# Down product in groups of 3, 4 and 4 blocks, its tiles laid out ahead of the last up pair, and the low parts of its first two items made between that pair's conv taps

## The chip, the cores and the metric

The kernel runs on one core of a Trainium2 chip. The metric is the time of one execution in device microseconds (us); lower is better. The version before the change takes 1487.21 us, the median of three runs (1486.26 to 1487.37).

A core has five engines that run their own instruction queues in order and wait for one another by semaphores: TensorE (PE; PEld is its weight load), VectorE (DVE), ScalarE (ACT), GpSimd (POOL) and SyncE (SP, here only a queue for DMA transfers).

## The reference

One layer of a streaming encoder over 1024 positions plus 16 meta tokens: attention and a state-space branch, then a gated feed-forward part with a causal depthwise convolution, then a final norm. The change lies in the last two, whose core is this:

```python
def _conv_ffn(xn, w_up, conv_w, conv_b, w_down):
    seq_len = xn.shape[1]
    hid = xn @ w_up
    hp = jnp.pad(hid, ((0, 0), (CONV_WIDTH - 1, 0), (0, 0)))
    conv = conv_b + sum(hp[:, j:j + seq_len] * conv_w[j] for j in range(CONV_WIDTH))
    val, gate = jnp.split(conv, 2, axis=-1)
    return (jax.nn.silu(gate) * val) @ w_down
...
        h = h + _conv_ffn(xn, w_ffn_up[layer], ffn_conv_w[layer], ffn_conv_b[layer],
                          w_ffn_down[layer])
    h = _rmsnorm(h, norm_final_g)
    return h[:, N_META:]
```

All is float32; `D_MODEL` is 1024 and `D_FF` 2816, so `w_up` has 2 x 2816 columns and `w_down` 2816 rows.

## The kernel before

**Split operands.** Float32 products are made of three matmuls. Each operand is split into a high part (a copy by ACT, rounded to the matmul's type) and a low part, the difference between the operand and the high part (`split_lo`, L127, on DVE or POOL). This difference is called a cut below. PE then adds high x high, high x low and low x high in PSUM.

**The up product** makes 22 pairs of 128 gate and 128 value rows. Pairs 0 and 21 are done plainly (`plain_pair`), pairs 1 to 20 by a seven-product scheme (`block_pair`). In a plain pair, three blocks of positions are computed for the gate (`og`) and then three for the value (`ov`). Behind each block ACT applies the first conv tap (L1034) and DVE the two others (L1036). `glue` (L1005) applies Silu, multiplies gate and value (on POOL, for the last pair on DVE, L1007), and writes the 128 rows to `a_d` in DRAM (from SP's queue, for the last pair from ACT's, L1008). While the up product runs, POOL also prepares sums of the down weights, `t_d`.

**The down product** takes the 22 x 128 rows of `a_d` as 11 blocks of two, and multiplies them by `w_down` with a Strassen-Winograd scheme of seven products, made in `ORDER` = (0, 4, 1, 2, 5, 3, 6). The blocks are worked off in groups: two blocks, then three, three and three. An item is one product of one group. For each item and block `forms` (before: L1142 to L1170) makes two operands: one from quarter tiles of `a_d` (`ar`, sometimes after a sum on POOL, L1151 to L1157), one from a weight tile (`wr`). Each is copied by ACT (L1163) and cut (L127), on POOL for products 0, 4 and 5 and on DVE for 1, 2, 3 and 6. The results lie in 14 operand slots: six of their own (`op0` to `op5`) and eight in the tiles `xhi` and `xlo`, which are free once the up product has ended.

`product` (L1206) then runs four tiles of 128 positions; per tile every block gives three matmuls of 512 columns (L1219 to L1221). PSUM banks are `m`, `m`, `m`, `po` or `s`, `t`, `s`, `t` in turn, and products 4, 5 and 6 add to the banks of 0, 1 and 3. Behind each tile its bank is drained: copied by ACT for the very first product (L1224), else added by DVE (L1226) to `hs` (the residual and result, read from `h_d`) or to a helper `u`. In the last group the norm follows: `square` (L1192: square and sum on ACT, `va` on DVE, L1195) and `finish` (L1198: a power on POOL, L1200, scaling on DVE, L1201, and ACT, L1203, then the write). The last tile of the last item is done in two pieces, of 288 and 224 columns, in one bank.

**What sets the order.** The program text gives the dependencies, and a scheduler sets the order of instructions on each engine at build time; `after(a, b)` (L122) puts `a` behind `b` on their engine or behind its end without data between them. `prepare` (L1253) prepares as many items ahead as the 14 slots allow. Before the change the pool `down1` with the first tiles of the down product is opened behind the last up pair (L1115), the rest (`dn`) further on, so the loads of the first blocks wait for the tiles of the up product to be freed. `first_copy` and `first_add` hold the cuts of group 0 behind certain drains, and `behind` puts loads behind those of `hs`.

Of the kernel before, what the change touches and what calls it, by code (L numbers as in the profile page):

```python
# [47 lines left out]
def block_kernel(ctx, tc, x, meta, g1, w_q, w_k, w_v, w_f, w_u, w_g, b_f, w_ao, lam_d, bw_d, cw_d,  # L48
# [912 lines left out]
    ha = pool(st_r, "hid", side="right")  # L961
# [20 lines left out]
    def combine(a, b, op):  # L982
        f_ = rp.tile([P, KH, P], F, tag="sf", name="sf", bufs=2)
        sums.append(GP.tensor_tensor(f_, a, b, op))  # L984
        return f_
# [19 lines left out]
    def glue(g_, v_, c):  # L1005
        S.activation(g_, g_, AF.Silu)  # L1006
        (V if c == NFF - 1 else GP).tensor_tensor(v_, v_, g_, ALU.mult)  # L1007
        (S if c == NFF - 1 else SY).dma_start(a_d[P * c:P * c + P], v_)  # L1008
# [4 lines left out]
    def plain_pair(c):  # L1013
# [3 lines left out]
        for m, tag in ((NFF + c, "og"), (c, "ov")):  # L1017
            raw = up_raw(m)
            w2 = [split_q(raw[:, KH * q:KH * q + KH]) for q in range(2)]
            if last:  # L1020
                o = ha.tile([P, SEQ], F, tag="h", name=tag, bufs=3, padded_shape=[P, LQ + 2])
            else:
                o = conv_out(m, tag)
            for t, n in QBLK:
# [9 lines left out]
                S.activation(o_, ps[:, :w], AF.Identity, bias=cwc(3, m), scale=cwc(0, m))  # L1034
                for j in (1, 2):
                    V.scalar_tensor_tensor(out=o_, in0=ps[:, j:w + j], scalar=cwc(j, m), in1=o_,  # L1036
                                           op0=ALU.mult, op1=ALU.add)
# [69 lines left out]
    st_t.close()  # L1107
    plain_pair(NFF - 1)
# [4 lines left out]


    down1 = pool(ctx, "down1", side="left")  # L1115
    small = [down1.tile([P, 4, 512], R, name=f"op{q}") for q in range(4)]
# [3 lines left out]
    dpool = {}  # L1120
    pairs = {}

    h_load = []

    def raw_tile(j, k, h_):
        if (k, h_) not in pairs.setdefault(j, {}):
            pairs[j][k, h_] = dpool[j % 4 // 2].tile([P, 512], F, tag=f"a{k}{h_}", name="ar", bufs=2)
        return pairs[j][k, h_]

    def behind(ld, j, p=None):  # L1130
        if h_load and (j in groups[1] or p in (2, 5, 3, 6) and j in groups[0]):
            after(ld, h_load[3 if p == 2 else -1])

    def load_pair(j):
        for k in range(2):
            c0 = P * (2 * j + k)
            for h_ in range(2):
                behind(SY.dma_start(raw_tile(j, k, h_), a_d[c0:c0 + P, 512 * h_:512 * h_ + 512]), j)

    n_op = [0]  # L1140
    own_w = {0: (0, 0), 4: (1, 0), 6: (1, 1)}

    def forms(p, j):
        r = pairs[j]
        b_ = down1.tile([P, 512], F, tag="w", name="wr", bufs=8)
        behind(SY.dma_start(b_, w_block(*own_w[p], j) if p in own_w else t_d[p][P * j:P * j + P]), j, p)

        a11, a21, a12, a22 = (r[k, h_] for k in range(2) for h_ in range(2))
        sub, add = ALU.subtract, ALU.add
        if p == 1:  # L1150
            GP.tensor_tensor(a11, a11, a21, sub)  # L1151
        elif p == 2:
            GP.tensor_tensor(a11, a22, a11, add)
        elif p == 3:
            GP.tensor_tensor(a21, a22, a21, sub)
        elif p == 6:
            GP.tensor_tensor(a11, a11, a12, sub)  # L1157
        slot = ops[n_op[0] % len(ops)]
        n_op[0] += 1
        a_ = (a11, a11, a11, a21, a12, a22, a11)[p]  # L1160
        eng = GP if p in (0, 4, 5) else V
        for q, src in ((0, a_), (2, b_)):
            hi = S.copy(slot[q], src)  # L1163
            if first_copy and j < 2 and p >= 5:
                after(hi, first_copy[1])
            cut = split_lo(eng, slot[q + 1], src, slot[q])
            cuts.setdefault((p, j), []).append(cut)
            if first_add and eng is V and j < 2 and p > 2:
                after(cut, first_add[1 if p == 3 else 3])
        return slot  # L1170

    first_add, first_copy = [], []
    cuts = {}

# [31 lines left out]
    def product(g, p, slots, first, last):  # L1206
        l_, r_ = HALF
        joins = p in JOINS
        for t, bk in enumerate(banks(g, p)):
# [5 lines left out]
            for c0, n in parts:  # L1215
# [7 lines left out]
                if first and p == 0:  # L1223
                    first_copy.append(S.copy(to, ps))  # L1224
                else:
                    first_add.append(V.tensor_tensor(to, to, ps, ALU.subtract if p in MINUS else ALU.add))  # L1226
                    if (g, p, t) == (1, 0, 3):
                        for cut in cuts[1, 3] + cuts[1, 4]:
                            after(cut, first_add[-1])
# [473 lines left out]
```

## Time and profile before

| What | Value |
|---|---|
| Time, median of 3 runs | 1487.21 us (1486.26 to 1487.37) |
| Profiled execution, its time | 1486.29 us |
| Profiled execution, its span | 1484.5 us |
| PE busy | 1450.3 us, 98% of the span |
| DVE busy | 1050.5 us, 71% |
| ACT busy | 690.8 us, 47% |
| POOL busy | 664.5 us, 45% |
| Mean granted clock of PE | 0.991 |
| Last matmul of the up product starts | 1248.63 us |
| First matmul of the down product starts | 1248.79 us |
| Last matmul of the down product starts | 1477.21 us |

The span runs from the first to the last instruction of the profiled execution. Times inside the trace count from its start. Durations on the engines come from the trace: "busy" is the sum of the durations of an engine's instructions, and "idle before" is the time in which it had nothing to do just ahead of an instruction, with the instruction that ended it. Instructions overlap at their ends (a matmul of 512 columns is shown as 0.39 us while the next starts after 0.23), so the step from start to start tells the pace. The granted clock is TensorE's share of full speed.

### The profile page before, as it was taken

What the parts mean: (1) busy time and instruction counts of PE and PEld (TensorE: products, weight loads), DVE (VectorE), ACT (ScalarE), POOL (GpSimd) and SP (SyncE); (2) the same over time, 40 slices, a digit from 0 to 9 for tenths busy, and PEclk for the clock granted to TensorE, in tenths of its full rate; (3) what the DMA queues carried; (4) which work ended last, traced back from release to release, by engine and by line L of the source; (5) the groups of instructions that cost most, each with busy time, mean ns of one, the idle gap of its engine ahead of it and who ended that gap; (6) DMA issues with size and microseconds to landing.
All of it is one profiled execution on the core that took longest, in us unless ns stands there. A gap on an engine that the chain in (4) does not pass through costs nothing.

```text
span 1484.5 us, 26303 instructions
## 1 busy us (share of the span) xinstructions
PE 1450.3 (98%) x9681; PEld 1362.9 (92%) x9681; DVE 1050.5 (71%) x2169; ACT 690.8 (47%) x1338; POOL 664.5 (45%) x759
## 2 busy tenths in 40 slices
PE   7999999999999999999999999999999999899997
PEld 6999999988999999999879999999999998678886
DVE  7989377862657676656255888888876665888785
ACT  5355565542646566532046544444444434444343
POOL 2101105741554556525021455555544416779766
PEclk8999999999999999999999999999999999999999
DMA  6455544441120212157134555667543216764412
GB/s 244 105 135 144 157 96 136 143 151 31 37 92 24 80 51 65 44 205 269 69 143 114 128 163 167 183 174 182 143 121 93 86 44 230 260 207 133 141 45 114
DMA packets 83364, 190.96 MB, mean 129 GB/s; under 512 B 13818, under 2 KB 26250, under 8 KB 82884
## 3 DMA queue, kind: packets, MB, share of 16 engines
q1 hardware_dynamic: 67604, 154.77, 31.9%
q0 software_dynamic: 9984, 24.45, 8.9%
q10 hardware_dynamic: 5648, 10.07, 1.9%
q8 instruction: 76, 1.25, 0.3%
q14 instruction: 52, 0.43, 0.1%
HBM read 146.98 MB, written 61.00 MB: 140 GB/s over the span
## 4 chain that ended last, share of the span: by engine, by line
PE 82%; DVE 6%; issue 3%; DMA 3%; ACT 2%; POOL 2%; SPq 0%; POOLq 0%; DVEq 0%; ACTq 0%
PE mm L149 5%; PE mm L148 5%; PE mm L147 5%; PE sp L212 5%; PE sp L211 5%; PE sp L213 5%; PE mm L213 3%; PE mm L211 3%; PE mm L212 3%; PE tp L213 3%; PE tp L211 3%; PE tp L212 3%; PE tp L682 3%; PE po L704 2%; PE po L703 2%
## 5 line engine op out<-in xcount | busy, mean ns | idle before, releaser
L147 PE MATMUL mm<-xhi,whi 128*128 128x342 f32 (+2 forms) x584 | 191.2, 328 | 1.5 <-DVE q L127 1.0
L148 PE MATMUL mm<-xlo,whi 128*128 128x342 f32 (+2 forms) x584 | 189.8, 325 | 1.1 <-DVE xlo L127 0.9
L149 PE MATMUL mm<-xhi,wlo 128*128 128x342 f32 (+2 forms) x584 | 189.6, 325 | 0.0
L1007 POOL TENSOR_TENSOR ov<-ov,og 128x1024 f32<-128x1024 f32 x21 | 51.4, 2449 | 152.7 <-ACT og L1006 151.6
L127 DVE TENSOR_TENSOR sw<-sf,sw 128x512 fp32r<-128x512 f32 x80 | 75.8, 947 | 54.1 <-ACT sw L976 53.8
L147 PEld LDWEIGHTS mm<-xhi,whi 128*128 128x128 f32 x584 | 111.0, 190 | 3.3 <-ACT xhi L178 1.2
L148 PEld LDWEIGHTS mm<-xlo,whi 128*128 128x128 f32 x584 | 111.0, 190 | 2.6 <-DVE xlo L127 1.9
L149 PEld LDWEIGHTS mm<-xhi,wlo 128*128 128x128 f32 x584 | 110.9, 190 | 0.3
L976 ACT CAST sw<-sf 128x512 fp32r<-128x512 f32 x80 | 50.0, 625 | 119.5 <-POOL sf L984 83.1
L984 POOL TENSOR_TENSOR sf<-raw 128x512 f32<-128x512 f32 x40 | 52.4, 1311 | 102.1 <-PE mm L897 53.2
L213 PE MATMUL mm<-xhi,sw 128*128 128x256 f32 (+1 forms) x320 | 90.4, 283 | 0.0
L211 PE MATMUL mm<-xhi,sw 128*128 128x256 f32 (+1 forms) x320 | 90.3, 282 | 0.0
L212 PE MATMUL mm<-xlo,sw 128*128 128x256 f32 (+1 forms) x320 | 90.1, 281 | 0.0
L689 ACT CAST th<-tp 128x256 fp32r<-128x256 f32 (+3 forms) x120 | 56.1, 472 | 60.9 <-PE tp L682 28.2
L127 DVE TENSOR_TENSOR tl<-tp,th 128x256 fp32r<-128x256 f32 (+3 forms) x120 | 65.1, 547 | 26.2 <-ACT th L689 24.8
L976 ACT CAST sw<-raw 128x512 fp32r<-128x512 f32 x68 | 41.9, 621 | 82.7 <-DMA raw<-in_w_up_dram 33.9
L1093 DVE SCALAR_TENSOR_TENSOR ov<-hv,cwt,ov 128x1024 f32<-128x1024 f32 x40 | 78.7, 1969 | 0.1
L984 POOL TENSOR_TENSOR sf<-raw,sf 128x512 f32<-128x512 f32 x40 | 65.1, 1626 | 25.1 <-DVE sw L127 25.1
L654 POOL TENSOR_SCALAR pt<-pt,nm 128x144 f32<-128x144 f32 (+4 forms) x72 | 51.0, 709 | 52.9 <-DVE nm L653 51.8
L652 ACT ACTIVATE pt<-pt,nm 128x144 f32<-128x144 f32 (+4 forms) x72 | 52.9, 735 | 26.7 <-DVE nm L651 26.2
L645 DVE CUSTOM_DVE_ANT_0 pt<-sp,fb 128x328 f32<-128x328 f32 (+8 forms) x112 | 46.4, 430 | 20.6 <-PE sp L640 12.3
L211 PEld LDWEIGHTS mm<-xhi,sw 128*128 128x128 f32 x320 | 60.5, 189 | 0.0
(621 smaller groups left out, 5350.3 us busy)
## 6 DMA issues: line engine op xcount, KB each, us to landing
raw<-in_w_up_dram SPq DMA_DIRECT2D x44, 512.0 KB, 3.6
t_d<-in_w_dn_dram POOLq DMA_DIRECT2D x44, 256.0 KB, 7.0
ar<-a_d SPq DMA_DIRECT2D x44, 256.0 KB, 4.9
wr<-t_d SPq DMA_DIRECT2D x44, 256.0 KB, 3.2
a_d<-ov SPq DMA_DIRECT2D x21, 512.0 KB, 2.6
wr<-in_w_dn_dram SPq DMA_DIRECT2D x33, 256.0 KB, 5.0
t_d<-in_w_dn_dram SPq DMA_DIRECT2D x22, 256.0 KB, 4.5
t_d<-t_d SPq DMA_DIRECT2D x22, 256.0 KB, 4.8
```

Source lines behind the costliest of these rows:

```text
L127: return eng.tensor_tensor(out_, src, hi.bitcast(F), ALU.subtract)
L147: yield PE.matmul(ps, whi[:, i, :], ahi[:, i], start=(i == 0), stop=False)
L148: yield PE.matmul(ps, whi[:, i, :], alo[:, i], start=False, stop=False)
L149: yield PE.matmul(ps, wlo[:, i, :], ahi[:, i], start=False, stop=(i == k - 1))
L211: PE.matmul(ps, a[0][:, i], bh, start=(i == 0 and not joins), stop=False, skip_group_check=True)
L212: PE.matmul(ps, a[0][:, i], bl, start=False, stop=False, skip_group_check=True)
L213: PE.matmul(ps, a[1][:, i], bh, start=False, stop=(i == kh - 1), skip_group_check=True)
L652: S.activation(pt[:n, :kc], pt[:n, :kc], AF.Exp, bias=nm[:n, 1:2], scale=0.125, accum_out=nm[:n, 2:3])
L689: S.copy(th[:kn, z:tw], tp[:kn, z:tw])
L976: S.copy(hi, src)
L984: sums.append(GP.tensor_tensor(f_, a, b, op))
L1093: V.scalar_tensor_tensor(out=o, in0=h_[:, j:SEQ + j], scalar=cwc(j, m), in1=o, op0=ALU.mult, op1=ALU.add)
```

## The change

It has five parts.

1. **Groups.** The blocks are worked off as 3, 4 and 4 instead of 2, 3, 3 and 3.
2. **Layout.** The pools of the up product that are no longer needed (`upf`, `tright`, `hid`) get a stack of their own, `st_f`, closed ahead of the last up pair. `down1` is opened there too, with all tiles that the first items need; the last pair's `og` and `ov` lie in it.
3. **Loads.** Quarter tiles of `a_d` are loaded product by product as they are used (`USES`), not by block; `behind` is gone. The rows of pairs 20 and 21 are written to `a_d` from POOL's queue. All eight `hs` loads stand behind the preparation of the first items.
4. **First items.** The cuts of the first two items, (0, 0) and (0, 4), go to DVE, and `after` puts them and their ACT copies behind the taps of the last up pair's blocks, three to a block, from the second block on. Nine slots are given out, so item (0, 1) is prepared there as well.
5. **Later cuts.** `product` gets the DVE cuts that `prepare` has made and puts a quarter of them behind the drain ahead of each of its four tiles; `first_copy` and `first_add` go.

```diff
+    st_f = ExitStack()
+    fp = pool(st_f, "upf", side="right")
...
-        (S if c == NFF - 1 else SY).dma_start(a_d[P * c:P * c + P], v_)
+        (GP if c >= NFF - 2 else SY).dma_start(a_d[P * c:P * c + P], v_)
...
+                if last:
+                    convs.append((first, tap))
...
     st_t.close()
+    st_f.close()
+    down1 = pool(ctx, "down1", side="left")
...
+    small = op_tiles(3, 6)
+    a_room("11")
+    a_room("01")
+    for tag in ("og", "ov"):
+        down1.tile([P, D], F, tag=tag, name=tag, padded_shape=[P, LQ + 2])
+    for q in range(8):
+        down1.tile([P, 512], F, tag="w", name="wr", bufs=8)
...
     plain_pair(NFF - 1)
...
+    USES = {0: ((0, 0),), 4: ((1, 0),), 1: ((0, 0), (0, 1)), 2: ((1, 1), (0, 0)), 5: ((1, 1),), 3: ((1, 1), (0, 1)),
+            6: ((0, 0), (1, 0))}
+
+    def forms(g, p):
+        early = g == 0 and p in ORDER[:2]
+        eng = GP if p in (0, 4, 5) and not early else V
+        for j in groups[g]:
+            for kh in USES[p]:
+                raw_tile(j, *kh)
...
+            for q, src in ((0, a_), (2, wr[q_])):
+                hi = S.copy(slot[q], src)
+                cut = split_lo(eng, slot[q + 1], src, slot[q])
+                if (g, p) == (0, 5):
+                    after(cut, sums[-1])
+                if early:
+                    i = 2 * len(groups[0]) * ORDER.index(p) + 2 * q_ + q // 2
+                    after(hi, convs[1 + i // 3][0])
+                    after(cut, convs[1 + i // 3][1])
+                if eng is V:
+                    mine.append(cut)
...
-    def product(g, p, slots, first, last):
+    def product(g, p, slots, first, last, cuts):
...
+                    if drains:
+                        for cut in cuts[len(cuts) * t // 4:len(cuts) * (t + 1) // 4]:
+                            after(cut, drains[-1])
+                    drains.append(V.tensor_tensor(to, to, ps, ALU.subtract if p in MINUS else ALU.add))
...
-    groups = [range(0, 2), range(2, 5), range(5, 8), range(8, 11)]
+    groups = [range(0, 3), range(3, 7), range(7, 11)]
...
+    room[0] = 9
+    new = prepare()
...
+    for c in range(KD):
+        SY.dma_start(hs[c], h_d[P * c:P * c + P])
+    room[0] = len(ops) - 9
     for g, p in items:
-        prepare()
-        if (g, p) == (0, 0):
-            for c in range(4, KD):
-                h_load.append(SY.dma_start(hs[c], h_d[P * c:P * c + P]))
+        new = prepare()
```

Up to the last up pair the order on every engine is unchanged. Three places behind that show how instructions move; a row is line, operation and tiles, and lines behind L910 shift by up to some 30 between the two programs.

First, DVE at the end of the last up pair, before. The L1036 rows are the taps of its blocks (`x2`: two in a row), L1007 the multiplication of gate and value, and the L127 rows are cuts of the third item, (0, 1):

```order
L1036 SCALAR_TENSOR_TENSOR ov_14891<-tp_14920,cwt_9276,ov_14891 128x342 x2
L1036 SCALAR_TENSOR_TENSOR ov_14891<-sp_14948,cwt_9276,ov_14891 128x340 x2
L1007 TENSOR_TENSOR ov_14891<-ov_14891,og_14798 128x1024
L1277 MEMSET eps_15035 128x1
L127 TENSOR_TENSOR op4_15033<-ar_14986,op4_15033 128x512
L127 TENSOR_TENSOR op4_15033<-wr_15081,op4_15033 128x512
L127 TENSOR_TENSOR op5_15060<-ar_14994,op5_15060 128x512
L127 TENSOR_TENSOR op5_15060<-wr_15088,op5_15060 128x512
```

The same place after the change; taps are L1040 here, `op3` to `op5` the slots of the second item and `xhi` those of the third:

```order
L1040 SCALAR_TENSOR_TENSOR ov_14928<-tp_14957,cwt_9276,ov_14928 128x342
L127 TENSOR_TENSOR op3_14799<-ar_15040,op3_14799 128x512
L127 TENSOR_TENSOR op4_14800<-ar_15042,op4_14800 128x512
L1040 SCALAR_TENSOR_TENSOR ov_14928<-tp_14957,cwt_9276,ov_14928 128x342
L127 TENSOR_TENSOR op5_14801<-ar_15044,op5_14801 128x512
L127 TENSOR_TENSOR op3_14799<-wr_15046,op3_14799 128x512
L127 TENSOR_TENSOR op4_14800<-wr_15048,op4_14800 128x512
L1040 SCALAR_TENSOR_TENSOR ov_14928<-sp_14985,cwt_9276,ov_14928 128x340
L127 TENSOR_TENSOR op5_14801<-wr_15050,op5_14801 128x512
L127 TENSOR_TENSOR xhi_91<-ar_15016,xhi_91 128x512
L1040 SCALAR_TENSOR_TENSOR ov_14928<-sp_14985,cwt_9276,ov_14928 128x340
L127 TENSOR_TENSOR xhi_91<-wr_15070,xhi_91 128x512
```

Cuts of the second item, which stood on POOL, and of the third now stand between the taps, some of them between the two taps of one block.

Second, DVE in products 2 and 5 of the last group, before. The L1226 rows that change `u` drain product 2, and those that change `hs` drain product 5; L1195 is `va` of the norm:

```order
L127 TENSOR_TENSOR xhi<-ar,xhi 128x512
L127 TENSOR_TENSOR xhi<-wr,xhi 128x512
L1226 TENSOR_TENSOR hs_15072<-hs_15072,po 128x512
L1226 TENSOR_TENSOR u_15066<-u_15066,sp 128x512
L1226 TENSOR_TENSOR u_15067<-u_15067,tp 128x512
L1226 TENSOR_TENSOR u_15068<-u_15068,sp 128x512
L1226 TENSOR_TENSOR u_15069<-u_15069,tp 128x512
L1226 TENSOR_TENSOR hs_15070<-hs_15070,mm 128x512
L1195 SCALAR_TENSOR_TENSOR va<-ss,eps 128x1
L1226 TENSOR_TENSOR hs_15065<-hs_15065,mm 128x512
```

The same place after the change, from the last drain of product 2 on (drains are L1257, `va` is L1223):

```order
L1257 TENSOR_TENSOR u_15130<-u_15130,po 128x512
L127 TENSOR_TENSOR op_14799<-a_16009,op_14799 128x512
L127 TENSOR_TENSOR op_14799<-wr,op_14799 128x512
L1257 TENSOR_TENSOR hs_15123<-hs_15123,sp 128x512
L127 TENSOR_TENSOR op_14800<-ar,op_14800 128x512
L127 TENSOR_TENSOR op_14800<-wr,op_14800 128x512
L1223 SCALAR_TENSOR_TENSOR va<-ss,eps 128x1
L1257 TENSOR_TENSOR hs_15124<-hs_15124,tp 128x512
L127 TENSOR_TENSOR op_14801<-ar,op_14801 128x512
L127 TENSOR_TENSOR op_14801<-wr,op_14801 128x512
```

The last cuts stood ahead of these drains and now stand between them, two to a drain, through both products.

Third, DVE in products 3 and 6 of the last group, where the results are finished (L1201), before:

```order
L1226 TENSOR_TENSOR hs_15072<-hs_15072,tp 128x512
L1201 SCALAR_TENSOR_TENSOR hs_15071<-hs_15071,rs,gfB 128x512
L1226 TENSOR_TENSOR hs_15061<-hs_15061,sp 128x512
L1195 SCALAR_TENSOR_TENSOR va<-ss,va 128x1
L1201 SCALAR_TENSOR_TENSOR hs_15072<-hs_15072,rs,gfB 128x512
L1226 TENSOR_TENSOR hs_15062<-hs_15062,tp 128x512
L1195 SCALAR_TENSOR_TENSOR va<-ss,va 128x1
L1201 SCALAR_TENSOR_TENSOR hs_15061<-hs_15061,rs,gfB 128x512
```

And after the change (`finish` is L1229; `hs_15123` is the first of the eight result tiles here, while above they are numbered from `hs_15061`):

```order
L1257 TENSOR_TENSOR hs_15123<-hs_15123,mm 128x512
L1223 SCALAR_TENSOR_TENSOR va<-ss,va 128x1
L1229 SCALAR_TENSOR_TENSOR hs_15123<-hs_15123,rs,gfB 128x512
L1257 TENSOR_TENSOR hs_15124<-hs_15124,mm 128x512
L1223 SCALAR_TENSOR_TENSOR va<-ss,va 128x1
L1229 SCALAR_TENSOR_TENSOR hs_15124<-hs_15124,rs,gfB 128x512
L1257 TENSOR_TENSOR hs_15125<-hs_15125,mm 128x512
L1223 SCALAR_TENSOR_TENSOR va<-ss,va 128x1
L1257 TENSOR_TENSOR hs_15126<-hs_15126,po 128x512
L1229 SCALAR_TENSOR_TENSOR hs_15125<-hs_15125,rs,gfB 128x512
```

Before, the drain of the next tile stood ahead of a tile's `finish`; now a tile's `finish` mostly stands ahead of the next drain.

More of the change, by code (lines that the diff above doesn't have):

```diff
@@ L982, in combine @@
     def combine(a, b, op):
-        f_ = rp.tile([P, KH, P], F, tag="sf", name="sf", bufs=2)
+        f_ = fp.tile([P, KH, P], F, tag="sf", name="sf", bufs=2)
         sums.append(GP.tensor_tensor(f_, a, b, op))
@@ L1020, in plain_pair @@
             if last:
-                o = ha.tile([P, SEQ], F, tag="h", name=tag, bufs=3, padded_shape=[P, LQ + 2])
+                o = down1.tile([P, SEQ], F, tag=tag, name=tag, padded_shape=[P, LQ + 2])
             else:
@@ L1107, in block_kernel, with op_tiles, a_room @@
     st_t.close()
+    st_f.close()
+    down1 = pool(ctx, "down1", side="left")
+    def op_tiles(a, b):
+        return [down1.tile([P, 4, 512], R, name=f"op{q}") for q in range(a, b)]
+    def a_room(kh):
+        for q in range(3):
+            down1.tile([P, 512], F, tag=f"a{kh}{q}", name="ar")
+    small = op_tiles(3, 6)
[5 more added lines that the diff above has]
+        down1.tile([P, 512], F, tag="w", name="wr", bufs=8)
+    a_room("00")
+    a_room("10")
+    small = op_tiles(0, 3) + small
     plain_pair(NFF - 1)
@@ L1119, in block_kernel @@
             for t_ in (xhi, xlo) for q in range(4)]
-    dpool = {}
-    pairs = {}
-    h_load = []
+    pairs, halves = {}, {}
     def raw_tile(j, k, h_):
         if (k, h_) not in pairs.setdefault(j, {}):
-            pairs[j][k, h_] = dpool[j % 4 // 2].tile([P, 512], F, tag=f"a{k}{h_}", name="ar", bufs=2)
-        return pairs[j][k, h_]
-    def behind(ld, j, p=None):
-        if h_load and (j in groups[1] or p in (2, 5, 3, 6) and j in groups[0]):
-            after(ld, h_load[3 if p == 2 else -1])
@@ L1134, in load_pair @@
[L1134 to L1138, printed above, removed]
+            if j % 4 < 3:
+                t_ = down1.tile([P, 512], F, tag=f"a{k}{h_}{j % 4}", name="ar")
+            else:
+                if k == 0:
+                    halves[j, h_] = (dn.tile([P, D], F, tag="a3", name="a3") if h_ else
+                                     down1.tile([P, D], F, tag="og", name="a3", padded_shape=[P, LQ + 2]))
+                t_ = halves[j, h_][:, 512 * k:512 * k + 512]
@@ L1140, in block_kernel @@
+            c0 = P * (2 * j + k)
+            SY.dma_start(t_, a_d[c0:c0 + P, 512 * h_:512 * h_ + 512])
+            pairs[j][k, h_] = t_
+        return pairs[j][k, h_]
     n_op = [0]
     own_w = {0: (0, 0), 4: (1, 0), 6: (1, 1)}
[L1143 to L1148, printed above, removed]
-        sub, add = ALU.subtract, ALU.add
[L1150 to L1170, printed above, removed]
@@ L1177, in block_kernel @@
+    drains = []
     JOINS = {4: 0, 5: 1, 6: 3}
@@ L1223, in product @@
                 if first and p == 0:
-                    first_copy.append(S.copy(to, ps))
+                    drains.append(S.copy(to, ps))
                 else:
[L1226 to L1229, printed above, removed]
+                    if drains:
+                        for cut in cuts[len(cuts) * t // 4:len(cuts) * (t + 1) // 4]:
+                            after(cut, drains[-1])
+                    drains.append(V.tensor_tensor(to, to, ps, ALU.subtract if p in MINUS else ALU.add))
                 if last and p == 6:
```

76 lines of the change are left out of this document (37 added, 39 removed).

## The prediction

> **What bounds the kernel now.** The page's first part says that TensorE is nearly always busy, so a change can only win where it stands still or runs at a lower clock. The windows view (length, then busy time and count of PE, PEld, DVE, ACT, POOL, then the granted clock) finds that place in the down product.
>
> ```profile
> PE 1450.3 (98%) x9681; PEld 1362.9 (92%) x9681; DVE 1050.5 (71%) x2169; ACT 690.8 (47%) x1338; POOL 664.5 (45%) x759
> ...
> 1248.70:1316.00 67.30, 58.45 (x233) 45.24 (x232) 54.00 (x58) 31.12 (x57) 59.33 (x41) 0.92 0.70 246
> 1316.00:1474.00 158.00, 157.53 (x693) 129.13 (x692) 127.81 (x158) 63.13 (x125) 123.41 (x90) 1.00 0.35 114
> 1380.00:1470.00 90.00, 90.00 (x397) 74.12 (x396) 65.34 (x87) 32.91 (x68) 69.70 (x53) 1.00 0.21 65
> 1308.00:1312.00 4.00, 1.02 (x5) 0.52 (x5) 4.00 (x4) 1.46 (x3) 4.00 (x3) 1.00 0.57 169
> 1312.00:1316.00 4.00, 4.00 (x11) 3.14 (x12) 4.00 (x6) 1.24 (x2) 4.00 (x4) 0.57 0.52 159
> ```
>
> The third window has no pause: 90.00 / 397 = 0.227 us for a matmul of 512 columns. At that pace the first stage's 233 matmuls take 52.9 of its 67.30 us, so **14.4 us are lost there**; the next 693 take 157.3 of 158.00. The waits of PE (total, times, longest) from 1248.7 us on name what ends the pauses:
>
> ```profile
> PE sp L1219 <- DVE u L1226: 3.0, 1, 3.0
> PE sp L1219 <- DVE hs L1226: 2.1, 1, 2.1
> PE tp L1219 <- DVE hs L1226: 1.8, 1, 1.8
> PE mm L1220 <- POOL op L127: 1.7, 1, 1.7
> PE mm L1219 <- ACT xhi L1163: 1.4, 1, 1.4
> PE mm L1219 <- DVE hs L1226: 0.4, 1, 0.4
> ```
>
> All but the 1.8 (the end, below) lie in the first stage. They are low parts not yet made, or drains that stand in DVE's queue behind low parts. The rest of the 14.4 is clock: behind the pause of 3.0 us the window 1312 to 1316 shows clock 0.57, and its 11 matmuls take 4.00 instead of 2.5 us, 1.5 more. The Trainium skill's page "TensorE: Matmul & The Clock Gate", section "What's actually happening", puts the fall to half rate after an idle window of about 3.4 us. The trace shows it after 2.98 us, so the measurement decides; by the page, each 1.5 us that I add for such a fall below would be nothing.
>
> **What the change removes.** A low part is a "cut" (L127). These rows give its price, by whether POOL works beside it, and that of a drain:
>
> ```profile
> 1253.72 0.69 DVE L127 TENSOR_TENSOR op<-ar,op 128x512 fp32r<-128x512 f32 x1 [1.10 <-issue]
> 1254.33 1.79 DVE L127 TENSOR_TENSOR op<-wr,op 128x512 fp32r<-128x512 f32 x1
> 1256.05 1.77 DVE L127 TENSOR_TENSOR op<-ar,op 128x512 fp32r<-128x512 f32 x1
> ...
> 1250.23 7.04 POOL L127 TENSOR_TENSOR op<-wr,op 128x512 fp32r<-128x512 f32 x4
> ...
> 1248.70:1316.00 67.30, 34.56 (x26) 38.99 (x27) 0.92 0.70 246
> 1316.00:1474.00 158.00, 72.17 (x63) 53.53 (x37) 1.00 0.35 114
> ...
> 1444.96 0.68 DVE L1226 TENSOR_TENSOR hs<-hs,po 128x512 f32<-128x512 f32 x1
> 1445.56 0.68 DVE L1226 TENSOR_TENSOR u<-u,sp 128x512 f32<-128x512 f32 x1
> ```
>
> A cut takes 0.69 us, but 1.77 when POOL runs its own (7.04 / 4 = 1.76 each). The fifth and sixth rows count the cuts alone, DVE's first: 34.56 / 26 = 1.33 on average in the first stage, 72.17 / 63 = 1.15 after it. A drain takes a step of 0.60. Where POOL never stops, a drain and two cuts take two such pairs, 3.54 us, since the drain runs beside POOL: (3.54 - 0.60) / 2 = 1.47 a cut. I call the mean cut **c** and take 1.40, between 1.33 and 1.47; its ends are 0.69 and 1.77. The Trainium skill's page "SBUF", section "🔬 SBUF: two separate sides", says that the pair of ports shared by DVE and GpSimd is an exclusive lock held for a whole instruction; the rows of 1.77 agree. By that rule, with POOL never idle, c is 1.47, and the sum below would be 1476.2 instead of 1473.9.
>
> The 12 cuts of the first two items now stand between the last up pair's taps (L1036 before), on DVE.
>
> ```profile
> 1245.90 1.18 DVE L1036 SCALAR_TENSOR_TENSOR ov<-tp,cwt,ov 128x342 f32<-128x342 f32 x2 [2.53 <-ACT ov L1034]
> 1249.66 1.18 DVE L1036 SCALAR_TENSOR_TENSOR ov<-sp,cwt,ov 128x340 f32<-128x340 f32 x2 [2.57 <-ACT ov L1034]
> 1250.88 1.74 DVE L1007 TENSOR_TENSOR ov<-ov,og 128x1024 f32<-128x1024 f32 x1
> ```
>
> Three cuts at 0.69 fit into each idle 2.5 us, so the up pair is not held; without that cover (1.77 each) a gap overruns by 2.8, once. Their data must come early: in the trace the loads ar<-a_d start at 1234.86, behind pair 20's write; now they wait for neither that write nor the last up pair. All other loads of group 0 have at least one whole product (36 x 0.227 = 8.2 us) of lead against these landing times:
>
> ```profile
> ar<-a_d SPq DMA_DIRECT2D x33, 256.0 KB, 5.3
> wr<-t_d SPq DMA_DIRECT2D x20, 256.0 KB, 4.1
> hs<-h_d SPq DMA_DIRECT2D x8, 512.0 KB, 7.9
> ```
>
> The eight hs loads stand in SP's queue behind weight loads that wait for cuts; their first user, the drain of the second item, comes in DVE's row after 10 more cuts, so near 1269 (1249.7 + 2.8 + 1.2 + 1.7, all worked out under B, and 10 x 1.40), more than 7.9 behind the issue. Pair 21's write moves to POOL's queue and waits there for DVE's multiplication, which ends at about 1255. Behind it stand one sum for item 2 and POOL's cuts of product 5, whose first reader starts five products from now (1281.5 on PE): nothing. Of the 14.4 I keep 0.4 for the step into the first product (the smallest wait above): **-14.0**.
>
> **What it adds in group 0 (B).** With three blocks instead of two DVE has 24 later cuts there. From 1249.7: up to four early cuts that spill behind (4 x 0.69), taps 1.18, multiplication 1.74, 14 drains that stand ahead of the last cut (8.4), 24 cuts: it ends at 1263.8 + 24c. The seventh product needs it at 1248.8 + 6 x 8.17 = 1297.8. At c = 1.40 it is ready at 1297.4, so **B = 0**; at 1.47 1.3 late, at 1.77 8.5 late. At 0.69 there is only slack. POOL's 30 operations up to the ninth item's last cut, at 1.76, end at 1308; PE wants them at 1317: nothing.
>
> **What it adds at the end (C).** The last group has four blocks, so a tile is 12 x 0.227 = 2.72 us on PE (2.04 before). In its products 2 and 5 each tile brings DVE a drain and two cuts, 0.60 + 2c = 3.40 at c = 1.40, and POOL has its 12 sums and 4 multiplications there:
>
> ```profile
> 1446.32 15.05 POOL L1236 TENSOR_TENSOR hs<-hs,u 128x512 f32<-128x512 f32 x12 [5.50 <-DVE u L1226]
> 1461.31 5.05 POOL L1242 TENSOR_TENSOR hs<-hs,gfB 128x512 f32<-128x512 f32 x4
> ```
>
> Seven steps from tile to tile gain 7 x 0.68 = 4.8 of lag; the step into product 3 has no cuts and takes 1.6, 1.1 less than PE's: 3.7. Then comes the chain of the output, tile after tile:
>
> ```profile
> 1472.97 0.68 DVE L1226 TENSOR_TENSOR hs<-hs,tp 128x512 f32<-128x512 f32 x1
> 1474.39 0.75 DVE L1201 SCALAR_TENSOR_TENSOR hs<-hs,rs,gfB 128x512 f32<-128x512 f32 x1 [0.66 <-POOL rs L1200]
> 1475.06 0.68 DVE L1226 TENSOR_TENSOR hs<-hs,sp 128x512 f32<-128x512 f32 x1
> 1475.65 0.15 DVE L1195 SCALAR_TENSOR_TENSOR va<-ss,va 128x1 f32<-128x1 f32 x1
> ...
> 1475.77 0.63 ACT L1193 ACTIVATE sq<-hs 128x512 bf16<-128x512 f32 x1 [0.66 <-DVE hs L1226]
> 1476.31 0.19 ACT L1193 ACTIVATION_READ_ACCUMULATOR sq<-hs 128x1 f32 x1
> 1476.47 0.72 ACT L1203 ACTIVATE hs<-hs,rs 128x512 f32<-128x512 f32 x1
> ...
> 1475.89 0.55 POOL L1200 TENSOR_TENSOR rs<-va,nhalf 128x1 f32<-128x1 f32 x1 [1.53 <-DVE va L1195]
> ...
> 1473.10 0.29 PE L1219 MATMUL tp<-op 128*128 128x288 f32 x1
> 1473.22 0.29 PE L1220 MATMUL tp<-op 128*128 128x288 f32 x1
> ...
> 1474.15 0.30 PE L1221 MATMUL tp<-xhi 128*128 128x288 f32 x1
> 1476.23 0.37 PE L1219 MATMUL tp<-op 128*128 128x224 f32 x1 [1.78 <-DVE hs L1226]
> ```
>
> Before, the next tile's drain stood ahead of a tile's va and finish, and a step took 1475.06 - 1472.97 = 2.09. Now drain, va and finish of one tile stand together in five of seven steps: drain to square 0.71, square and its sum 0.73, va 0.03, va to POOL 0.24, POOL to finish 0.58, finish to the next drain 0.67 (1474.39 to 1475.06): 2.96. Two keep the drain ahead (1.6 each). Of the five, the last has only the finish left between (1.4) and one waits about 0.6, because its square stands in ACT's queue behind the copy (0.72) of the tile before: 3 x 2.96 + 3.56 + 2 x 1.6 + 1.4 = 17.0. PE's way over the same stretch is six tiles and 12 matmuls of 288 columns at 0.13, 17.9. So 0.9 of the lag is made up and 2.8 stays. The last 12 short matmuls wait for that drain plus 0.55 (its 0.45 and the signal), 3.4 us, where 1.8 stands now: **C = +1.6**, in general 14c - 18.0, and no less than -1.2 (the wait cannot fall below 0.55). More short matmuls cover the same columns, and the work behind them is the same: nothing.
>
> **Sum.** 1486.29 (profiled run, span 1484.5) - 14.0 + 0 + 1.6 = 1473.9. That run lies 0.9 under the median 1487.21, so the median of after may lie at 1473.9 to 1474.8: I say 1474.4.
>
> **Rivals.**
> 1. POOL leaves DVE alone: c up to 1.15, the mean after 1316: the lag is 0.2 ahead of the chain, and none behind it. B = 0, C = -1.2: 1471.1. For it: POOL's early cuts are gone. Against: its 30 operations run beside DVE's.
> 2. **DVE becomes the bound** of group 0: c from 1.5 to 1.66. At 1.6: B = 4.4, one slow clock spell 1.5, C = 4.4: 1482.6; at 1.5 (B 2.0, C 3.0) 1477.3. For it: DVE was 80% busy there (54.00 of 67.30) and still late.
> 3. **Slower:** POOL and DVE alternate without a break. c = 1.77: item 2's last cut comes 3.1 late, the seventh product's 8.5; two slow spells, 3.0; C = 6.8: 18.3 against 14.0, 1490.6. It decides from c = 1.66 on. Against: drains lie between cuts, and the mean was 1.33 under the same load. By the clock page's rule the 3.0 would go, and this would be 1487.6.
> 4. The change doesn't do what it says: the early operands land only after the last tap, and the 12 cuts come there at 1.40. The first item's six hold PE until about 1250.9 + 8.4, less the 2.5 us that its first tiles can do: 8 late, so 1481.9. Against: the loads start some 15 us before, and land in 5.3.
>
> **How the numbers follow.** Forecast 0.61 (c 1.25 to 1.5, 1472 to 1477.3), rival 1 0.12, rival 2 0.17, rival 3 0.05, rival 4 0.05. The range 1470.8 to 1481.5 leaves out rival 3, most of 4 and the upper end of 2. About 0.2%, 3 us, is what a measurement here can tell from no change: slower needs over 1490.2 (rival 3's end, 0.03), the same has its rest and rival 2's top (0.05), faster 0.92.
>
> **What would show it.** Right: PE has no pause over 1 us and clock 1.00 from 1248.8 to 1306; DVE's cuts stand before 1249.7; the mean cut of DVE in group 0 is 1.3 to 1.47; one wait of about 3.4 us ahead of the 224-column matmuls. Wrong: a pause at the third, fourth or seventh product that ends with a DVE cut (rivals 2 and 3), one at the first product that ends with a cut (rival 4), an end wait under 1 us (rival 1) or over 5, or any pause in the up pairs, which I take as unchanged.

## The result, and the profile after

The changed kernel takes 1476.32 us (median of 4 runs, 1475.52 to 1476.51), the kernel before 1487.12 us (4 runs): a ratio of 0.9927, 95% interval 0.991 to 0.9945, 10.8 us less. The profiled execution took 1475.52 us with a span of 1473.7 us.

Three windows of the kernel after: the first two are the stages shown of before, the third a piece of the end (columns as before).

```profile
1248.70:1316.00 67.30, 67.30 (x298) 55.48 (x297) 60.07 (x63) 34.17 (x64) 60.53 (x40) 1.00 0.73 255
1316.00:1458.00 142.00, 142.00 (x628) 116.99 (x627) 117.77 (x130) 58.27 (x114) 117.72 (x80) 1.00 0.37 117
1464.00:1467.00 3.00, 2.75 (x12) 2.64 (x12) 1.27 (x4) 1.67 (x5) 0.55 (x1) 0.50 0.50 189
```

In the first stage PE now makes 298 matmuls where it made 233, without a pause and at clock 1.00: the 14.4 us are gone whole. The list of PE's waits from the last up pair to the end has one line left:

```profile
PE po L1247 <- DVE hs L1257: 5.7, 1, 5.7
```

The timeline of PE (start, duration, what) shows where it lies:

```profile
1458.26 0.30 PE L1249 MATMUL po<-xhi 128*128 128x288 f32 x1
...
1464.25 0.55 PE L1247 MATMUL po<-op 128*128 128x224 f32 x1 [5.70 <-DVE hs L1257]
...
1466.74 0.41 PE L1249 MATMUL po<-xhi 128*128 128x224 f32 x1
```

The balance of the two profiled executions: the last matmul of 288 columns starts 15.9 us earlier (1474.15 to 1458.26). From there to the first of 224 columns it takes 5.99 us instead of 2.08, 3.9 more. The 12 short matmuls run 0.21 us apart, where nine ran about 0.11 apart: 2.5 us from the first to the last instead of 1.0, 1.5 more (0.3 of it for the three more matmuls, 1.2 for the clock of 0.50). The rest to the end of the span is 0.3 shorter. 15.9 - 3.9 - 1.5 + 0.3 = 10.8.

### The profile page after: what moved, and what is told of

Its sections match the earlier page's. It is cut to its first block, busy times and chain, and to the rows that moved or that the text cites. A ratio compares the mean times of both kernels' runs of the same rounds, so it can differ in the third digit from the quotient of the medians.

```text
span 1473.7 us, 26226 instructions
## 1 busy us (share of the span) xinstructions
PE 1446.6 (98%) x9684; PEld 1363.5 (93%) x9684; DVE 1051.1 (71%) x2153; ACT 691.0 (47%) x1338; POOL 659.6 (45%) x749
## 4 chain that ended last, share of the span: by engine, by line
PE 92%; DVE 2%; DMA 2%; issue 2%; ACT 1%; POOL 1%; SPq 0%; POOLq 0%; ACTq 0%; DVEq 0%
PE mm L149 6%; PE mm L148 6%; PE mm L147 6%; PE sp L212 5%; PE sp L211 5%; PE sp L213 5%; PE tp L213 3%; PE tp L211 3%; PE mm L213 3%; PE mm L211 3%; PE tp L212 3%; PE mm L212 3%; PE tp L682 3%; PE mm L1247 2%; PE mm L1249 2%; PE mm L1248 2%
## 5 line engine op out<-in xcount | busy, mean ns | idle before, releaser
L127 DVE TENSOR_TENSOR sw<-sf,sw 128x512 fp32r<-128x512 f32 x80 | 73.8, 923 | 53.9 <-ACT sw L978 53.8
L127 DVE TENSOR_TENSOR tl<-tp,th 128x256 fp32r<-128x256 f32 (+3 forms) x120 | 65.2, 547 | 25.7 <-ACT th L689 24.4
```

The source lines that it names most:

```text
L127: return eng.tensor_tensor(out_, src, hi.bitcast(F), ALU.subtract)
```

## The experiments

Each makes one edit to the changed kernel, but for two that add a second edit to an earlier one, and one that runs a kernel again. All ran beside the kernel before; the ratio is to that, and the medians are of four runs where no number is given. The kernel before took 1487.1 to 1488.0 us beside them, so a difference of under 1 us to the changed kernel says nothing.

### The cuts behind the taps instead of between them

```diff
-                    after(hi, convs[1 + i // 3][0])
-                    after(cut, convs[1 + i // 3][1])
+                    after(hi, convs[5][0])
+                    after(cut, convs[5][1])
```

> The changed kernel, but all copies and cuts of the first two items are put behind the taps of the last block of the last up pair, instead of three to a block. Theory (the taps' idle time carries the gain of the first items): the 12 cuts and the multiplication stand in a row from 1250.9 us on, at 1.40 us each, the first item's six hold PE until about 1257 to 1259, and the second item's six come late again: two or three pauses, 8 to 11 us in all with a slow clock spell, so 1485 to 1488 us. Rival (early loads and the layout alone carry it, the place of the cuts is nothing): pauses under 2 us in all, 1476 to 1478.5 us.

Measured: 1486.89 us (10 runs), ratio 0.9994 (0.9984 to 1.0003). Its waits of PE:

```profile
PE po L1246 <- DVE hs L1256: 6.2, 1, 6.2
PE mm L1247 <- DVE op L127: 3.3, 2, 3.1
PE mm L1246 <- ACT op L1189: 1.7, 1, 1.7
```

The window behind the longest pause of the first stage:

```profile
1259.00:1263.00 4.00, 3.40 (x8) 2.73 (x9) 4.00 (x5) 1.80 (x4) 2.72 (x2) 0.50 1.00 366
```

The first item waits 1.7 us for a high part, and then 3.1 us for a cut; clock 0.50 follows. The second item is not late again, so there are fewer pauses than expected, but with the slow matmuls behind them it costs 10.6 us, as much as the theory said, and nearly the whole gain. Taken together, early tiles, early loads and the new groups bring nothing that can be measured without the cuts between the taps: the first stage still makes 259 matmuls where it made 233 before, but the wait at the end is 6.2 us instead of 1.8, and this takes the gain back.

### The groups of before

```diff
-    groups = [range(0, 3), range(3, 7), range(7, 11)]
+    groups = [range(0, 2), range(2, 5), range(5, 8), range(8, 11)]
```

> The changed kernel with the groups of before, 2, 3, 3 and 3 blocks. Theory (a product of three blocks gives DVE the time that a product of two does not): in group 0 DVE has 16 later cuts and 14 drains, ready near 1255.4 + 16 x 1.40 + 8.4 = 1286 us, while the seventh product wants them at 1248.8 + 6 x 5.44 = 1281.5: some 4.7 us of pauses and 1.5 of slow clock there; the end is shorter (tiles of 2.04 us, three quarters of the cuts), a wait of 2 to 4 us instead of 5.7 and no slow spell: 1476 to 1480 us in all. Rival (the layout and the early cuts carry the gain, the size of the groups only costs at the end): no pause over 1 us in group 0 and 1471 to 1473 us.

Measured: 1480.14 us (1478.38 to 1482.24), ratio 0.9948 (0.9933 to 0.9962), 3.8 above the changed kernel. Its waits of PE:

```profile
PE mm L1247 <- DVE hs L1257: 5.0, 1, 5.0
PE tp L1247 <- DVE hs L1257: 4.2, 1, 4.2
```

DVE's timeline around the end of the first:

```profile
1267.07 3.42 DVE L127 TENSOR_TENSOR xlo<-wr,xlo 128x512 fp32r<-128x512 f32 x2
1270.40 0.68 DVE L1257 TENSOR_TENSOR hs<-hs,mm 128x512 f32<-128x512 f32 x1
```

One pause of 5.0 us stays in group 0, as large as the theory said, but at the fourth product and not at the seventh: that product needs a bank whose drain stands in DVE's queue behind the cuts of later items. With products of 5.4 instead of 8.2 us PE comes back to the bank too early. So the larger first group carries part of the gain. Its end, with tiles of three blocks, waits 4.2 us, just over the 2 to 4 that were expected, and the short matmuls behind it run 0.21 us apart, the slow clock that was not expected there.

### Writes of pairs 20 and 21 from the queues of before

```diff
-        (GP if c >= NFF - 2 else SY).dma_start(a_d[P * c:P * c + P], v_)
+        (S if c == NFF - 1 else SY).dma_start(a_d[P * c:P * c + P], v_)
```

> The changed kernel, but the rows of pair 20 are written from SP's queue and those of pair 21 from ACT's, as before. The write of pair 20 then stands ahead of the first loads of the down product, which start near 1234.5 instead of 1219.1 us. Theory (the loads have to start ahead of that write only by the time that 12 of them take): the operands land from 1238 to 1246 us, the cuts shift by 1 to 3 us, no pause over 1 us: 1476 to 1478 us. Rival (the early loads are what lets the cuts stand between the taps): the first or second item is late by 3 to 6 us, 1479.5 to 1484 us.

Measured: 1476.85 us (1476.73 to 1478.26), ratio 0.9928 (0.9911 to 0.9945): the same as the changed kernel. Its waits of PE:

```profile
PE po L1247 <- DVE hs L1257: 6.2, 1, 6.2
PE sp L1247 <- DVE u L1257: 0.9, 1, 0.9
```

No pause over 1 us arises in the first stage. That the first loads get ahead of pair 20's write is not needed: they then start 14.8 us later, at 1233.93 instead of 1219.10, and still come in time.

### The early cuts on POOL

```diff
-        eng = GP if p in (0, 4, 5) and not early else V
+        eng = GP if p in (0, 4, 5) else V
```

> The changed kernel, but the 12 cuts of the first two items stay on POOL, where before had them, still three to a block behind the taps. Theory (the gain is that they stand early, on whichever engine has room; POOL takes 1.3 to 1.77 us for one, 16 to 21 us for 12, and has eight sums beside them): the second item's last cut ends at 1257 to 1262 us where PE wants it at 1257, a pause of 0 to 4 us: 1476 to 1480 us. Rival (DVE's faster cut is what carries the gain): pauses of over 5 us at the first and second item, 1482 us and more.

Measured: 1484.71 us (10 runs), ratio 0.9977 (0.9967 to 0.9986), 8.4 above the changed kernel. Its waits of PE:

```profile
PE po L1247 <- DVE hs L1257: 6.0, 1, 6.0
PE sp L1249 <- DVE xhi L127: 4.2, 1, 4.2
```

POOL's and DVE's timelines, the sums of the third item and the cut that PE waits for:

```profile
1260.78 3.44 POOL L1178 TENSOR_TENSOR ar<-ar 128x512 f32<-128x512 f32 x2
...
1264.90 6.62 DVE L127 TENSOR_TENSOR xhi<-ar,xhi 128x512 fp32r<-128x512 f32 x1
```

Neither expectation had the place. The last early cut ends where this sum starts, at 1260.8, as the theory said, and costs no pause that the list shows. But POOL's sums for the third item (L1178) now stand among and behind its cuts, to 1264.2, and DVE's cut of that item comes to stand beside POOL's next row of operations, where it takes 6.6 us. PE pauses 4.2 us for it and goes on at half pace. So the engine matters: with the cuts on DVE, POOL has the third item's sums done early.

### The end: finish behind the next drain, on DVE alone

```diff
+        after(fin, drains[-1])
...
-                finish(4 + t, l_, r_)
+                todo.append(4 + t)
...
+                while todo:
+                    finish(todo.pop(), l_, r_)
```

(`fin` is the scaling on DVE in `finish`; `todo` holds a tile until the next one is drained.)

> The changed kernel, but in the last two products each tile's finish is put behind the next tile's drain on DVE. Theory (the serial chain drain, square, va, finish keeps the lag that the cuts have made): the step falls from 2.96 to about 2.1 us, PE's tile takes 2.72, so of the lag of about 6 us ahead of product 3 some 4.3 are made up; the wait ahead of the 224-column matmuls falls from 5.7 to about 2.2 us and the 12 short matmuls run at 0.11 instead of 0.21: 1470.5 to 1472.5 us. Rival (the lag comes from the cuts alone and the chain is bound by ACT or POOL whatever stands on DVE): the wait stays over 4.5 us and the time within 1.5 us of 1476.3.

Measured: 1475.73 us (1475.46 to 1475.87), ratio 0.9917 (0.9902 to 0.9932), 0.6 below the changed kernel, which can't be told from none. A miss: a wait of 5.3 us stays, as the rival had it. ACT's timeline shows why:

```profile
1450.07 0.73 ACT L1232 ACTIVATE hs<-hs,rs 128x512 f32<-128x512 f32 x1 [0.86 <-POOL rs L1228]
1450.82 0.37 ACTq L1233 DMA_DIRECT2D out_dram<-hs  x1
1451.24 0.63 ACT L1221 ACTIVATE sq<-hs 128x512 bf16<-128x512 f32 x1 [0.45 <-DVE hs L1229]
```

The next tile has been drained at 1449.99, but its square starts at 1451.24, behind the copy and the write of the tile before (issuing the write, 0.37 us, is not counted as busy, so the list shows it as idle time and names DVE). The step is 2.76 us instead of 2.96. One order on one queue was loosened, and the other queue kept it.

### The end: the same on ACT

```diff
+        after(S.activation(hs[c][:, a], hs[c][:, a], AF.Copy, scale=rs), squares[-1])
```

(With the edit before; `squares` holds the squares, and the next tile's is made ahead of `finish`.)

> The changed kernel with the last run's edit (each finish behind the next drain on DVE) and the same on ACT: the finish's copy stands behind the next tile's square. Theory (the step of 2.76 us that stayed is ACT's: the copy of 0.72 and its write stand ahead of the next square): the step falls to 1.7 to 2.1 us against PE's 2.72, the lag of 6 us ahead of product 3 is made up almost wholly, the last wait is 0.6 to 1.5 us with no slow clock behind it: 1469.5 to 1471.5 us. Rival (the power on POOL or the lag of the cuts holds it): the wait stays over 4 us, within 1.5 us of 1476.3.

Measured: 1471.48 us (1470.91 to 1471.96), ratio 0.9887 (0.9872 to 0.9902), 4.8 below the changed kernel. Its wait of PE:

```profile
PE po L1248 <- DVE hs L1258: 1.5, 1, 1.5
```

Two drains in a row on DVE's timeline:

```profile
1452.73 0.68 DVE L1258 TENSOR_TENSOR hs<-hs,mm 128x512 f32<-128x512 f32 x1
...
1454.49 0.68 DVE L1258 TENSOR_TENSOR hs<-hs,po 128x512 f32<-128x512 f32 x1
```

The step is 1454.49 - 1452.73 = 1.76 us, well under PE's tile of 2.72, and the lag is made up on the way.

### The 12 sums of product 2 on DVE

```diff
-                    GP.tensor_tensor(d_, d_, u2[t], op)
+                    V.tensor_tensor(d_, d_, u2[t], op)
```

> The changed kernel, but the 12 sums behind product 2 of the last group are made by DVE instead of POOL. DVE gets 12 x 0.60 = 7.2 us more work in products 2 and 5. Theory (the lag there comes from cuts that wait for POOL's sums: 1.18 and 1.77 us instead of 0.69, and 1.24 for va): cuts of products 2 and 5 fall to 0.6 to 0.8 us, the lag ahead of product 3 from 6 to 1 to 3 us in spite of the added work, the last wait from 5.7 to 0.6 to 2.5 us: 1470 to 1473 us. Rival (DVE has simply too many operations per tile, contention apart): the lag grows by about 7 us, and the time to 1480 or more.

Measured: 1472.02 us (1470.07 to 1473.04), ratio 0.9889 (0.9874 to 0.9904), 4.3 below the changed kernel. Its wait of PE:

```profile
PE po L1247 <- DVE hs L1257: 2.3, 1, 2.3
```

The cuts in products 2 and 5 (a window of L127 alone, DVE's busy time and count first):

```profile
1420.00:1441.10 21.10, 10.56 (x14) 0.00 (x0) 1.00 0.00 1
```

10.56 / 14 = 0.75 us a cut. DVE has 7.2 us more work there, and yet its first drain of product 3 starts at 1442.93 us, where the changed kernel had 1446.67: what it lost beside POOL's sums was more than the sums themselves cost it.

### The cuts of the last group not held behind drains

```diff
-                    if drains:
+                    if drains and not last:
```

> The changed kernel, but in the last group the cuts are not held behind the drains, so the scheduler puts them earlier, four or five together, ahead of product 5's drains. Theory (two cuts to each drain beside POOL's sums are what makes the lag): the last cuts are done ahead of product 5, the lag ahead of product 3 falls below 3 us, the wait to 0.6 to 3 us: 1470.5 to 1473.5 us. Rival (the same work in another order): the drains of product 2 come as much later as the cuts come earlier, the sums on POOL start later too, and the wait stays at 4.5 to 7 us: 1475 to 1478 us.

Measured: 1476.71 us (1473.69 to 1477.29), ratio 0.9918 (0.9903 to 0.9933), the same as the changed kernel. Its waits of PE:

```profile
PE mm L1247 <- DVE u L1257: 4.9, 1, 4.9
PE po L1247 <- DVE hs L1257: 0.5, 1, 0.5
```

The last wait falls to 0.5 us, as the theory said, but a pause of 4.9 us comes up at product 4 of this group (from 1393.9 us on), and the time stays. The pause waits for a drain of product 0, and this stands in DVE's queue behind cuts that are late because one of them had a strange duration. The timelines of DVE and POOL:

```profile
1373.18 11.52 DVE L127 TENSOR_TENSOR op<-a,op 128x512 fp32r<-128x512 f32 x1
...
1384.78 1.67 POOL L1180 TENSOR_TENSOR a<-a,a 128x512 f32<-128x512 f32 x1 [0.62 <-DVE op L127]
```

The time is where the rival had it, though not for its reason. A cut that takes 0.69 us alone stood 11.5 us. POOL went through nine operations beside it, one every 1.26 us as if alone, and the cut ended when POOL had to wait for it. Two more runs were made to tell whether that is chance, and whether the pause comes from it.

### The same kernel once more

> The run with the last group's cuts free once more, unchanged, to see whether DVE's long cut comes again. Theory (POOL keeps the shared way to memory while it has work without a wait, so the order of instructions decides it): the same cut stands 9 to 13 us again, with a pause of 4 to 6 us at the next product. Rival (a chance of one execution): that cut takes under 2 us and the pause is gone, near 1471 us.

Measured: 1478.89 us in a single run. The same cut on DVE's timeline:

```profile
1375.61 11.10 DVE L127 TENSOR_TENSOR op<-a,op 128x512 fp32r<-128x512 f32 x1
```

Its longest wait of PE is 4.5 us, at the same place as before. The long cut came in both executions that were profiled, so it is not a chance of one: it goes with this order of instructions.

### Free cuts in products 2 and 5 alone

```diff
-                    if drains:
+                    if drains and not (last and p in (2, 5)):
```

> As the run with the last group's cuts free, but free only for the cuts that stand in products 2 and 5; those in the products before stay behind their drains, as in the changed kernel. In the run before, one cut of product 1's item stood 11.5 us in DVE's row at 1373.2 us, while POOL went through nine operations without a gap, and the drains behind it were late. Theory (that cut made the pause of 4.9 us; the cuts ahead of product 2's drains cost PE nothing): the cut stands a group's length from it, no pause over 1 us, the last wait at 0.5 to 1.5 us without slow clock: 1469.5 to 1472 us. Rival (the same work in another order: what leaves the end holds PE ahead of it): a pause of 3 to 6 us ahead of the end, 1474.5 to 1478 us.

Measured: 1476.76 us (1476.05 to 1477.59), ratio 0.9925 (0.9909 to 0.9942), the same as the changed kernel. Its wait of PE:

```profile
PE po L1247 <- DVE hs L1257: 5.4, 1, 5.4
```

POOL's sums of product 2 and first power, and DVE's first finish, on their timelines:

```profile
1428.68 16.86 POOL L1264 TENSOR_TENSOR hs<-hs,u 128x512 f32<-128x512 f32 x12 [6.05 <-DVE u L1257]
...
1450.52 0.56 POOL L1228 TENSOR_TENSOR rs<-va,nhalf 128x1 f32<-128x1 f32 x1
...
1451.11 0.75 DVE L1229 SCALAR_TENSOR_TENSOR hs<-hs,rs,gfB 128x512 f32<-128x512 f32 x1 [3.04 <-POOL rs L1228]
```

Half the theory held: the long cut is gone at that place (1.26 us), and the pause at product 4 with it. The other half fell. The wait at the end is back with 5.4 us: the cuts stand ahead of product 2's drains, POOL's sums start only at 1428.68 (1419.95 in the changed kernel), and the first power, which every finish needs, stands behind them and the four multiplications to 1450.52. DVE waits 3.0 us for it. So with the sums on POOL this other order brought nothing either. The run before probably had its short wait at the end because PE had already lost 4.9 us ahead of it; no run shows that by itself.

### Both cures together

The kernel with both edits of the end on DVE and ACT, and the sums on DVE.

> The changed kernel with both cures of its end: finish and copy behind the next tile on DVE and ACT, and the 12 sums of product 2 on DVE. Alone they left a last wait of 1.5 and 2.3 us. Theory (the lag of the cuts and the serial chain are the two parts of one wait): with both the wait is at its floor of 0.5 us and no slow clock follows, 1 us less than the first alone: 1469.5 to 1471.5 us. Rival (DVE's added 7.2 us cost elsewhere what they spare): a new pause in products 2 and 5 and 1472 us or more.

Measured: 1469.32 us (1468.8 to 1470.18), ratio 0.9878 (0.9862 to 0.9895), 7.0 below the changed kernel and just under the expected range, in an execution with this list of waits:

```profile
PE po L1248 <- DVE hs L1258: 0.5, 1, 0.5
```

The down product runs without a pause from its first matmul to the last 288-column one, and then waits 0.5 us. This version beats both kernels.

## Why the prediction was right

The forecast was 1474.4 us, measured are 1476.32, inside the range and on its upper side. That it came so close is partly luck. Two terms were off, in opposite directions: 1.9 us more than forecast were gained ahead of the end, and 3.5 us more were lost there.

Of the signs named ahead, these came: no pause over 1 us and clock 1.00 up to 1306 us, no pause in the last up pair, and one wait ahead of the 224-column matmuls. These did not: the mean cut of group 0 lies under 1.3 to 1.47, the last early cut ends after 1249.7, and the wait at the end, 5.7 us, lies over the 5 that was named as a sign of being wrong.

**What bounds the kernel; the 14.4 us.** Right. All waits of the first stage are gone, and the clock with them. The 0.4 us kept for the step into the first product did not stay, nor did the 0.7 us of the stage behind it. Up to the last matmul of 288 columns 15.9 us were gained where 14.0 were forecast; some 0.3 of that is the later place of the split (12 instead of 9 short matmuls follow), and 0.5 is left unexplained. The forecast named one slow spell in the first stage before. There were two: the windows 1271 to 1275 and 1275 to 1279 show a granted clock of 0.55 and 0.60 as well. As both are gone, this did not harm the sum.

**The early cuts.** The mechanism was right, and the two experiments on it show that the place (10.6 us) and the engine (8.4, because POOL's own sums come late) both carry it. The cover was worse than thought. This is DVE's timeline after:

```profile
1251.84 0.56 DVE L1040 SCALAR_TENSOR_TENSOR ov<-sp,cwt,ov 128x340 f32<-128x340 f32 x1
1252.32 0.68 DVE L127 TENSOR_TENSOR op<-wr,op 128x512 fp32r<-128x512 f32 x1
...
1258.86 2.32 DVE L1009 TENSOR_TENSOR ov<-ov,og 128x1024 f32<-128x1024 f32 x1
```

The last block's taps start 2.2 us later than before, and the last of the 12 early cuts ends between them, at 1253.0. The multiplication starts at 1258.86, where the forecast has 1253.6, behind cuts of the third item. PE does not wait for it: pair 21's rows are needed only in the last group.

**B, group 0.** Right at 0, with more slack than forecast. The cuts of group 0 after (L127 alone, DVE's busy time and count first), and the last of DVE's later cuts on its timeline:

```profile
1248.70:1298.00 49.30, 33.75 (x30) 24.24 (x15) 1.00 0.88 314
...
1292.70 0.68 DVE L127 TENSOR_TENSOR xhi<-wr,xhi 128x512 fp32r<-128x512 f32 x1
```

The mean cut there is 33.75 / 30 = 1.13 us, less than the 1.40 taken, and the last one ends at 1293.4 instead of 1297.4. POOL was busy for 43.40 of these 49.30 us; why it cost DVE less than forecast was not tried.

**Loads and queues.** Right at nothing; the writes could have stayed on their queues.

**C, the end.** Forecast +1.6, measured 3.9 + 1.5 - 0.3 = +5.1 (4.8 without the 0.3 of the later split). The chain of seven steps was right to a tenth (1463.75 - 1446.67 = 17.1, forecast 17.0), as was a tile with two cuts (3.40). The term that was mis-sized is the lag ahead of the chain. These are drains, and the cuts and the `va` of product 5, after:

```profile
1419.20 0.67 DVE L1257 TENSOR_TENSOR u<-u,mm 128x512 f32<-128x512 f32 x1
...
1428.89 0.68 DVE L1257 TENSOR_TENSOR u<-u,po 128x512 f32<-128x512 f32 x1
...
1432.29 0.67 DVE L1257 TENSOR_TENSOR hs<-hs,sp 128x512 f32<-128x512 f32 x1
1432.89 1.18 DVE L127 TENSOR_TENSOR op<-ar,op 128x512 fp32r<-128x512 f32 x1
1433.99 1.77 DVE L127 TENSOR_TENSOR op<-wr,op 128x512 fp32r<-128x512 f32 x1
1435.69 1.24 DVE L1223 SCALAR_TENSOR_TENSOR va<-ss,eps 128x1 f32<-128x1 f32 x1
1436.85 0.67 DVE L1257 TENSOR_TENSOR hs<-hs,tp 128x512 f32<-128x512 f32 x1
...
1441.52 0.68 DVE L1257 TENSOR_TENSOR hs<-hs,sp 128x512 f32<-128x512 f32 x1
...
1446.67 0.68 DVE L1257 TENSOR_TENSOR hs<-hs,mm 128x512 f32<-128x512 f32 x1
...
1463.75 0.45 DVE L1257 TENSOR_TENSOR hs<-hs,po 128x288 f32<-128x288 f32 x1
```

A tile of product 2 takes 1432.29 - 1428.89 = 3.40 us, as forecast. In product 5 a `va` is added, one number in each partition, and it takes 1.24 us beside POOL's sums (0.15 without): two tiles take 4.56 and 4.67. The forecast counted the `va` there as nothing, though the step of 2.96 had one. From product 2's first drain at 1419.20 to product 3's first at 1446.67 are 27.5 us, PE's eight tiles of 2.72 are 21.8: the lag gains 5.7 instead of 3.7 us, the wait is 5.7 instead of 3.4. The experiment with the sums on DVE shows that POOL's sums beside them make the cuts long (0.75 us on average without them); the two with free cuts show that another order of the same work doesn't help.

The other part is the clock. The forecast counted a slow spell behind a long pause in its rivals for group 0, but not at the end, where the last 12 matmuls run at 0.50. It costs 1.2 us: they take 2.5 us from first to last, and 1.3 in the run with both cures.

**The rivals.** Rival 1's price came in group 0 (1.13 us a cut, where it had up to 1.15), but its end did not: the wait is 5.7 us, not under 1. DVE as the bound of group 0 (rivals 2 and 3) did not come; at the end DVE is what PE waits for, as the forecast had it. Late early operands (rival 4) did not come, not even with loads that start 14.8 us later.

**Clock and contention.** Behind the pause of 5.70 us at the end the granted clock is 0.50, and the short matmuls run 0.21 us apart instead of 0.11. The Trainium skill's page "TensorE: Matmul & The Clock Gate", section "What's actually happening", has the fall to half rate after an idle window of about 3.4 us, and the trace agrees. The prediction says that by this rule both slow spells of rival 3 would go. That is a misreading: of its delays, 3.1 and 8.5 us, the second is longer than the window even when the first is taken off.

Shorter pauses can show the fall too. Before, it came behind 2.98 us. In the run with the sums on DVE the pause is 2.31 us; ten of the short matmuls behind it run 0.11 us apart, and then the clock falls while PE works (PE's timeline, and a window):

```profile
1460.86 0.37 PE L1247 MATMUL po<-op 128*128 128x224 f32 x1 [2.31 <-DVE hs L1257]
...
1462.07 0.38 PE L1248 MATMUL po<-xhi 128*128 128x224 f32 x1
1462.25 0.41 PE L1249 MATMUL po<-xhi 128*128 128x224 f32 x1
...
1462.00:1463.00 1.00, 0.66 (x5) 0.39 (x3) 0.95 (x2) 0.72 (x1) 0.02 (x1) 0.54 0.08 27
```

So that pause cost almost nothing because the work behind it was nearly done when the clock fell, and these runs give no shortest pause that is safe.

A `va` of 0.15 us takes 1.24 beside POOL. The Trainium skill's page "SBUF", section "🔬 SBUF: two separate sides", has DVE and GpSimd share a pair of ports under a lock that is held for a whole instruction, and the `va` agrees with it. The 1.77 us that the prediction took as the upper end of a cut came from DVE and POOL taking turns; single cuts of 6.6 to 11.5 us show that it was no bound.

## What to carry to other kernels

Look for the idle time of the engine that is late, not of the one that is bound: here the gain hung on preparing the next stage's operands in the gaps of the stage before (10.6 of 10.8 us were lost without it), and on doing it on DVE, since POOL's own work for the next item came late when it had those cuts too. Where DVE and POOL share a stretch, count every DVE operation that can wait for POOL, the tiny ones too: giving DVE the POOL's work can be faster than letting both run. A chain of tiles over several queues is held by the slowest of them: reordering DVE alone brought 0.6 us, DVE and ACT together 4.8.

## What was not expected of the hardware

A cut on DVE can stand until POOL, which goes through its operations without a gap, has to wait for it: 6.96 us in the changed kernel, 6.62 with the early cuts on POOL, 11.52 and 11.10 in the two runs of one experiment. In the changed kernel PE has no wait there, so it costs nothing. The long cut at that place, the first of a tile `a`, is no chance: all eleven traces with groups of 3, 4 and 4 have it, between 1306 and 1318 us, at 6.6 to 9.9 us; the two with groups of 2, 3, 3 and 3 have no cut over 3 us in the down product. DVE's and POOL's timelines in the changed kernel:

```profile
1307.04 6.96 DVE L127 TENSOR_TENSOR op<-a,op 128x512 fp32r<-128x512 f32 x1
...
1314.09 1.68 POOL L1180 TENSOR_TENSOR a<-a,a 128x512 f32<-128x512 f32 x1 [0.63 <-DVE op L127]
```

Elsewhere the two engines take turns, a cut at 1.77 us and a POOL operation at 1.7. What decides between the two was not tried.

The operation on 128 x 1 numbers lost as much beside POOL (1.24 us for 0.15) as a cut of 128 x 512 (1.77 for 0.69). And 12 sums moved from POOL to DVE, 7.2 us of work, made DVE 3.7 us earlier at product 3.
